# Rotary embedding on one core: loads and stores change queues, and the late loads wait between ScalarE's copies

## Chip, cores, metric

One core of a Trainium2 chip (trn2). The metric is the device time of one execution in microseconds (us), lower is better.

## The reference

```python
# x: (16, 512, 1024) float32, cos and sin: (512, 32), num_heads = 16
x = x.reshape(batch, seq, num_heads, head_dim)          # heads of 64
x1, x2 = x[..., :32], x[..., 32:]
rotated = concatenate([x1*cos - x2*sin, x1*sin + x2*cos], axis=-1)
```

33.5 MB are read and 33.5 MB are written, with three operations per element between them.

## The kernel before, as far as the change touches it

The kernel cuts the input into 64 "rows" of 128 partitions x 1024 floats and ten transfers ("tiles"): batches 0, 1, 14 and 15 alone (4 rows each), the other twelve in pairs (8 rows each). A ring of slots in SBUF, the on-chip memory, holds 40 rows; a row is computed in place and stored from its slot. So six loads can start at once, and four (rows 40 to 47, 48 to 55, 56 to 59, 60 to 63) reuse slots and must wait for a store.

Per row, VectorE multiplies by cos into PSUM, the memory that TensorE adds into (three slots), GpSimd makes the product of the swapped halves with sin into SBUF (in the fourth row of each pair: VectorE), and the sum is made by VectorE, or, in 21 rows, by TensorE adding into PSUM and ScalarE copying the result to the slot.

```python
        def on_sync(sp):                       # SyncE: all loads
            for t, (b, n) in enumerate(tiles):
                if b * R1 % R2 == 0 and b * R1 >= RING:
                    k = (b * R1 - RING) // R2
                    sp.wait_ge(sem_out[k], 16 * stores_of(k))
                sp.dma_start(in_sbuf(t), in_dram(x1, x2, t)).then_inc(sem_in[t], 16)
                ...                            # after the first: the two tables
            sp.wait_ge(sem_rest, ...)

        def on_scalar(ae):                     # ScalarE: tables, copies, all stores
            ...
            for u in range(NU):
                t, r, k = where(u)
                if PE2[u]:
                    ae.wait_ge(sem_e, n_pe[u])
                    ae.activation(xs[:, k, :], t1_ps[:, u % NT1, :], COPY).then_inc(sem_a, 1)
                if r == tiles[t][1] - 1:
                    wait_added(ae, u)
                    k = u // R2
                    ae.dma_start(in_dram(o1, o2, t), in_sbuf(t)).then_inc(sem_out[k] if k < EARLY else sem_rest, 16)

            # VectorE's product of row u waits until PSUM slot u % 3 is free:
                    if PE2[v]:                 # v = u - 3
                        ve.wait_ge(sem_a, n_pe[v])
```

## Time and profile before

| | before |
|---|---|
| timed, median | 161.3 us |
| profiled run | 167.47 us (span 166.1) |
| bytes moved, mean rate over the profiled span | 67.26 MB, 405 GB/s |
| busy: GpSimd, VectorE, TensorE, ScalarE | 136.6, 130.5, 72.6, 24.0 us |

The profiled run was 3.8% above the timed ones. In rows of busy tenths each digit is one of 40 equal slices of the span, 9 is 90% or more. A timeline line reads: start, duration, engine, line of the program, operation, and in brackets the idle time before it and what ended it. "ACTq" and "SPq" are the queues that issue transfers. A transfer lands when the last part of its completion is in. "Room" is idle time that a delay can use up before anything after it moves.

### The profile page before, as it was taken

Reading aid. Unit: us, or ns where it says so; the run is one execution under the profiler, and the core shown is the slowest. Engines: PE = TensorE matmul, PEld = TensorE weight load, DVE = VectorE, ACT = ScalarE, POOL = GpSimd, SP = SyncE. Lnnn points to the kernel's source line nnn. Section 1 sums busy time; section 2 is a strip of 40 time slices with the busy share of each in tenths; the row PEclk is TensorE's granted clock in tenths of the full one; section 3 lists DMA queues with packets and bytes.
Section 4 is the critical chain, followed back from the end, with each engine's and each line's share of the span. In section 5 each row is a group of like instructions: output and inputs, shape, how many; then the busy total and the mean of one; then the engine's idle time right before and its main releaser. Section 6 shows DMA issues by size and latency. Waiting matters only on the chain.

```text
span 166.1 us, 568 instructions
## 1 busy us (share of the span) xinstructions
PE 72.6 (44%) x94; PEld 24.6 (15%) x94; DVE 130.5 (79%) x117; ACT 24.0 (14%) x26; POOL 136.6 (82%) x67
## 2 busy tenths in 40 slices
PE   6040006196629371924292909381193827800000
PEld 1020002041202011301130213020130212200000
DVE  0069997798999999999999899972999997069600
ACT  3020000204022201222022011302022022110000
POOL 5059999999999999999999799962999999069500
PEclk9999999957696975599659555955559555595555
DMA  5999999999999999999989999999999999999293
GB/s 158 427 425 458 450 391 426 462 391 418 446 489 387 444 434 403 482 363 412 466 387 482 395 403 466 395 442 426 403 478 426 387 422 458 442 395 434 107 383 142
DMA packets 3170, 67.26 MB, mean 405 GB/s; under 512 B 352, under 2 KB 608, under 8 KB 608
## 3 DMA queue, kind: packets, MB, share of 16 engines
q1 hardware_dynamic: 1728, 33.69, 48.3%
q10 hardware_dynamic: 1440, 33.56, 47.3%
q14 instruction: 2, 0.02, 0.0%
HBM read 33.69 MB, written 33.55 MB: 405 GB/s over the span
## 4 chain that ended last, share of the span: by engine, by line
DMA 52%; POOL 15%; issue 11%; DVE 8%; PE 6%; ACT 1%; SPq 1%; POOLq 0%; DVEq 0%; ACTq 0%
DMA x_sb<-in_x_dram 33%; DMA out_dram<-x_sb 19%; POOL t_sb L254 15%; PE t_ps L209 6%; DVE x_sb L301 4%; DVE t_ps L290 4%; ACT x_sb L175 1%; SPq L156 1%; SPq L159 1%; DVE t_sb L283 0%; DVEq L300 0%; POOLq L145 0%; POOLq L143 0%; ACTq L136 0%
## 5 line engine op out<-in xcount | busy, mean ns | idle before, releaser
L254 POOL TENSOR_TENSOR t_sb<-x_sb,s_sb 128x1024 f32<-128x1024 f32 x58 | 134.2, 2355 | 18.7 <-DMA x_sb<-in_x_dram 11.7
L209 PE MATMUL t_ps<-t_sb,ident 128*128 128x512 f32 x84 | 67.8, 966 | 65.3 <-POOL t_sb L254 45.1
L290 DVE TENSOR_TENSOR t_ps<-x_sb,pair_ps 128x1024 f32<-128x1024 f32 x48 | 57.9, 1222 | 8.1 <-DMA x_sb<-in_x_dram 4.8
L301 DVE TENSOR_TENSOR x_sb<-t_ps,t_sb 128x1024 f32<-128x1024 f32 x43 | 52.4, 1220 | 2.7 <-POOL t_sb L254 2.5
L209 PEld LDWEIGHTS t_ps<-t_sb,ident 128*128 128x128 f32 x84 | 22.7, 295 | 109.6 <-issue 62.1
L175 ACT ACTIVATE x_sb<-t_ps 128x1024 f32<-128x1024 f32 x21 | 21.5, 1024 | 112.0 <-PE t_ps L209 112.0
L290 DVE TENSOR_TENSOR t_ps<-x_sb,tab_ps 128x1024 f32<-128x1024 f32 x16 | 19.3, 1222 | 7.1 <-DMA x_sb<-in_x_dram 6.7
L283 DVE TENSOR_TENSOR t_sb<-x_sb,tab_ps 128x1024 f32<-128x1024 f32 x6 | 7.3, 1215 | 0.0
L261 DVE COPY tab_ps<-stage 128x128 f32<-128x128 f32 x1 | 0.3, 295 | 8.1 <-DMA stage<-in_cos_dram 8.1
L192 PE MATMUL pair_ps<-stage,pick 128*128 128x256 f32 x4 | 2.0, 664 | 5.6 <-DMA stage<-in_sin_dram 5.6
L185 PE MATMUL t_ps<-zero 128*128 128x512 bf16 x6 | 2.7, 630 | 1.3 <-DVE zero L259 1.3
L192 PEld LDWEIGHTS pair_ps<-stage,pick 128*128 128x128 f32 x4 | 1.2, 322 | 6.6 <-issue 6.4
L235 POOL TENSOR_SCALAR_AFFINE_SELECT pick<-pick 128x128 f32<-128x128 f32 x2 | 1.4, 706 | 0.1
L165 ACT ACT_TABLE_LOAD x1 | 1.3, 1283 | 0.8 <-PEq L334 0.8
L165 ACT ACTIVATE s_sb<-stage 128x128 f32<-128x128 f32 x1 | 0.3, 309 | 7.4 <-DMA stage<-in_sin_dram 7.4
L185 PEld LDWEIGHTS t_ps<-zero 128*128 128x128 bf16 x6 | 0.7, 137 | 2.4 <-DVE zero L259 1.2
L259 DVE MEMSET zero<- 128x256 uint32 x1 | 0.3, 272 | 0.9 <-PEq L334 0.9
L169 ACT ACTIVATE s_sb<-pair_ps 128x256 f32<-128x256 f32 x1 | 0.4, 384 | 1.7 <-PE pair_ps L192 1.7
L220 POOL MEMSET ident<- 128x128 f32 x1 | 0.2, 205 | 0.3 <-POOLq L334 0.3
L170 ACT ACTIVATE s_sb<-pair_ps 128x256 f32<-128x256 f32 x1 | 0.4, 377 | 0.0
L222 POOL TENSOR_SCALAR_AFFINE_SELECT ident<-ident 128x128 f32<-128x128 f32 x1 | 0.3, 297 | 0.1
L334 POOL MEMSET const-float32-0.0<- 128x1 f32 x1 | 0.1, 99 | 0.3 <-issue 0.3
(7 smaller groups left out, 1.3 us busy)
## 6 DMA issues: line engine op xcount, KB each, us to landing
x_sb<-in_x_dram SPq DMA_DIRECT2D x6, 4096.0 KB, 39.3
out_dram<-x_sb ACTq DMA_DIRECT2D x6, 4096.0 KB, 30.4
x_sb<-in_x_dram SPq DMA_DIRECT2D x4, 2048.0 KB, 24.3
out_dram<-x_sb ACTq DMA_DIRECT2D x4, 2048.0 KB, 17.6
stage<-in_cos_dram SPq DMA_DIRECT2D x1, 64.0 KB, 8.0
stage<-in_sin_dram SPq DMA_DIRECT2D x1, 64.0 KB, 7.7
```

What stands on the lines that cost most here:

```text
L156: sp.dma_start(in_sbuf(t), in_dram(x1, x2, t)).then_inc(sem_in[t], 16)
L159: sp.dma_start(stage[:, i, :], table.rearrange("(s r) d -> s (r d)", r=R1)).then_inc(sem, 16)
L165: ae.activation(s1_sb[:, :, 0, :], sv, COPY, scale=-1.0)
L175: ae.activation(xs[:, k, :], t1_ps[:, u % NT1, :], COPY).then_inc(sem_a, 1)
L185: pe.matmul(t1_ps[:, k, b * BANK:(b + 1) * BANK], zero[:, 0:P], zero[:], start=True, stop=True).then_inc(sem_w, 1)
L192: pe.matmul(pair_ps[:, k].rearrange("p c r d -> p (c r d)"), pick[:, k].rearrange("q s b -> q (s b)"), stage[:].rearrange("q c f -> q (c f)"),
L209: ins = pe.matmul(t1_ps[:, u % NT1, b * BANK:(b + 1) * BANK], ident[:], t2[:, b * BANK:(b + 1) * BANK], start=False, stop=True, skip_group ...
L235: pl.affine_select(out=pick[:, k], in_=pick[:, k], compare_op=mybir.AluOpType.is_equal, fill=0.0, base=-k, pattern=[[-2, P // 2], [0, 2]], ...
L254: pl.tensor_tensor(t2_sb[:, u % NT2, :, :, :], swapped(k), over_heads(s_of(t, r)), mult).then_inc(sem_p, 1)
L283: ve.tensor_tensor(t2_sb[:, u % NT2, :, :, :], swapped(k), over_heads(v_ps), mult)
L290: ve.tensor_tensor(t1_ps[:, u % NT1, :].rearrange("p (h d) -> p h d", d=HALF), x_sb[:, k, :, :, :].rearrange("p h t d -> p (h t) d"), c_of ...
L301: ve.tensor_tensor(xs[:, k, :], t1_ps[:, u % NT1, :], t2_sb[:, u % NT2, :, :, :].rearrange("p h t d -> p (h t d)"), add,).then_inc(sem_v, 1)
```

## The change

Intent: swap the two queues, so that the engine with no arithmetic (SyncE) issues each store the moment its rows are ready, and ScalarE, which only has copies, issues the loads. The late loads and their waits come into ScalarE's program after the copy of the row that lies LAG = 10 rows behind the last row of the store that frees the slots. That is after rows 17, 25 and 33 (two loads).

```diff
+    LAG = 10
         def on_sync(sp):
+            for u in range(NU):
+                t, r, k = where(u)
+                if r == tiles[t][1] - 1:
+                    wait_added(sp, u)
+                    ...
+                    sp.dma_start(in_dram(o1, o2, t), in_sbuf(t)).then_inc(...)
         def on_scalar(ae):
+            later = {}
             for t, (b, n) in enumerate(tiles):
-                    sp.wait_ge(sem_out[k], 16 * stores_of(k))
+                if b * R1 + n <= RING:
+                    load(ae, t)
+                else:
+                    later.setdefault((b * R1 - RING) // R2 * R2 + R2 - 1 + LAG, []).append(t)
             ...
             for u in range(NU):
                 if PE2[u]:
                     ...                              # the copy, as before
-                if r == tiles[t][1] - 1:             # the store, now on SyncE
+                for t in later.get(u, ()):
+                    k = (tiles[t][0] * R1 - RING) // R2
+                    ae.wait_ge(sem_out[k], 16 * stores_of(k))
+                    load(ae, t)
```

No instruction of the other three engines changes.

More of the change, by code (lines that the diff above doesn't have):

```diff
@@ L149, in stores_of, with load, on_scalar @@
             return sum(b * R1 // R2 == k for b, _ in tiles)
+        def load(eng, t):
+            eng.dma_start(in_sbuf(t), in_dram(x1, x2, t)).then_inc(sem_in[t], 16)
         def on_sync(sp):
+            for u in range(NU):
+                t, r, k = where(u)
+                if r == tiles[t][1] - 1:
+                    wait_added(sp, u)
+                    k = u // R2
+                    sp.dma_start(in_dram(o1, o2, t), in_sbuf(t)).then_inc(sem_out[k] if k < EARLY else sem_rest, 16)
+            sp.wait_ge(sem_rest, 16 * sum(stores_of(k) for k in range(EARLY, NU // R2)))
+        def on_scalar(ae):
+            later = {}
             for t, (b, n) in enumerate(tiles):
-                if b * R1 % R2 == 0 and b * R1 >= RING:
-                    k = (b * R1 - RING) // R2
-                    sp.wait_ge(sem_out[k], 16 * stores_of(k))
-                sp.dma_start(in_sbuf(t), in_dram(x1, x2, t)).then_inc(sem_in[t], 16)
+                if b * R1 + n <= RING:
+                    load(ae, t)
+                else:
+                    later.setdefault((b * R1 - RING) // R2 * R2 + R2 - 1 + LAG, []).append(t)
                 if t == 0:
                     for i, (table, sem) in enumerate(((cos, sem_cos), (sin, sem_sin))):
-                        sp.dma_start(stage[:, i, :], table.rearrange("(s r) d -> s (r d)", r=R1)).then_inc(sem, 16)
-            sp.wait_ge(sem_rest, 16 * sum(stores_of(k) for k in range(EARLY, NU // R2)))
-        def on_scalar(ae):
+                        ae.dma_start(stage[:, i, :], table.rearrange("(s r) d -> s (r d)", r=R1)).then_inc(sem, 16)
             ae.wait_ge(sem_sin, 16)
@@ L171, in on_scalar @@
             for u in range(NU):
-                t, r, k = where(u)
                 if PE2[u]:
                     ae.wait_ge(sem_e, n_pe[u])
-                    ae.activation(xs[:, k, :], t1_ps[:, u % NT1, :], COPY).then_inc(sem_a, 1)
-                if r == tiles[t][1] - 1:
-                    wait_added(ae, u)
-                    k = u // R2
-                    ae.dma_start(in_dram(o1, o2, t), in_sbuf(t)).then_inc(sem_out[k] if k < EARLY else sem_rest, 16)
+                    ae.activation(xs[:, u % RING, :], t1_ps[:, u % NT1, :], COPY).then_inc(sem_a, 1)
+                for t in later.get(u, ()):
+                    k = (tiles[t][0] * R1 - RING) // R2
+                    ae.wait_ge(sem_out[k], 16 * stores_of(k))
+                    load(ae, t)
         def on_tensor(pe):
```

## The prediction

> **What bounds the kernel now.** I read the page's share of busy time by slice first, then the chain of waits, then the timelines of the issuing queues, of ScalarE and of VectorE around the four late loads.
>
> The page, busy tenths by slice (40 slices of 4.15 us):
>
> ```profile
> DVE  0069997798999999999999899972999997069600
> POOL 5059999999999999999999799962999999069500
> DMA  5999999999999999999989999999999999999293
> GB/s 158 427 425 458 450 391 426 462 391 418 446 489 387 444 434 403 482 363 412 466 387 482 395 403 466 395 442 426 403 478 426 387 422 458 442 395 434 107 383 142
> ```
>
> The DMA row is full from slice 2 to slice 37, about 2 to 153 us. DVE and POOL are nearly full too, but show holes at slices 28 and 35. So the transfers lead, and the arithmetic follows with a little room. Only the last three slices are something else: a tail of arithmetic and one store.
>
> The end of that tail, from the timelines of VectorE, of GpSimd and of ScalarE's queue:
>
> ```profile
> 130.36 1.22 DVE L290 TENSOR_TENSOR t_ps<-x_sb,pair_ps 128x1024 f32<-128x1024 f32 x1
> 131.51 1.23 DVE L290 TENSOR_TENSOR t_ps<-x_sb,tab_ps 128x1024 f32<-128x1024 f32 x1
> ...
> 146.65 2.36 DVE L290 TENSOR_TENSOR t_ps<-x_sb,tab_ps 128x1024 f32<-128x1024 f32 x2 [6.66 <-DMA x_sb<-in_x_dram]
> ```
> ```profile
> 146.70 9.27 POOL L254 TENSOR_TENSOR t_sb<-x_sb,s_sb 128x1024 f32<-128x1024 f32 x4 [5.85 <-DMA x_sb<-in_x_dram]
> ```
>
> The last load (batch 15, rows 60 to 63) is complete at 146.65. VectorE had stood idle 6.66 us for it and GpSimd 5.85. After it come four GpSimd products (9.27 us), one addition (1.22) and the last store, issued at 157.38 and complete at 166.02. So the span is the landing of the last load plus 19.4 us, and the room in front of it is 5.85 us on GpSimd.
>
> **What the change touches.** The kernel holds 40 of 64 rows. Four loads reuse slots: batches 10 and 11 (rows 40 to 47), 12 and 13 (48 to 55), 14 (56 to 59) and 15 (60 to 63). They wait for the stores of rows 0 to 7, 8 to 15 and, the last two, 16 to 23. The queue's own waits on SyncE and its timeline give the moments:
>
> ```profile
> SPq L156 <- DMA out_dram<-x_sb: 88.3, 3, 49.6
> ```
> ```profile
> 55.21 0.54 SPq L156 DMA_DIRECT2D x_sb<-in_x_dram  x1
> ```
> ```profile
> 75.55 0.53 SPq L156 DMA_DIRECT2D x_sb<-in_x_dram  x1
> ```
> ```profile
> 94.96 1.48 SPq L156 DMA_DIRECT2D x_sb<-in_x_dram  x2
> ```
>
> SyncE waits 88 us in all, which is free, as it has nothing else to do; every late load starts as soon as its store has landed. In the new kernel ScalarE does these waits, between copies that other engines need. Its timeline now (copies are of rows 6, 9, 11, 14, 17, 19, 22, 25, 27, 30, 33, 35 and so on, counted off in order):
>
> ```profile
> 53.05 1.02 ACT L175 ACTIVATE x_sb<-t_ps 128x1024 f32<-128x1024 f32 x1 [5.50 <-PE t_ps L209]
> 55.41 1.02 ACT L175 ACTIVATE x_sb<-t_ps 128x1024 f32<-128x1024 f32 x1 [1.34 <-PE t_ps L209]
> ...
> 69.45 1.02 ACT L175 ACTIVATE x_sb<-t_ps 128x1024 f32<-128x1024 f32 x1 [6.38 <-PE t_ps L209]
> 71.69 1.02 ACT L175 ACTIVATE x_sb<-t_ps 128x1024 f32<-128x1024 f32 x1 [1.22 <-PE t_ps L209]
> ...
> 85.63 1.02 ACT L175 ACTIVATE x_sb<-t_ps 128x1024 f32<-128x1024 f32 x1 [7.40 <-PE t_ps L209]
> 88.29 1.02 ACT L175 ACTIVATE x_sb<-t_ps 128x1024 f32<-128x1024 f32 x1 [1.64 <-PE t_ps L209]
> ```
>
> These are rows 17 and 19, 25 and 27, 33 and 35. The new waits stand after rows 17, 25 and 33, that is, in the three short gaps.
>
> **What the Trainium skill says.** "DMA: Bandwidth & Descriptors", section Issuing engines are not separate DMA queues: transfers from either engine end on the same 16 DMA engines and interleave, and a second issuer saves issue time only. The trace agrees that issue is small: 0.34 to 0.61 us on ScalarE's queue, 0.34 to 1.10 on SyncE's, for transfers that take 8 to 69 us to land. So swapping the two queues should not change the rate. The same page, section Anatomy of one DMA: a semaphore wait happens on the issuing sequencer before dispatch. "Perfetto Trace Analysis", section Tensor Engine Instruction, says that ScalarE is strictly first in, first out. Together: a ScalarE that waits for a store cannot start the next copy. The trace of before can't show that for loads, as ScalarE waits for no transfer after the tables. "ScalarE: Activation LUTs", section What ACT_TABLE_LOAD costs, gives about 1283 ns for a table load; the trace has 1.28 us.
>
> **The change part by part.**
>
> Removed: ten store issues from ScalarE, about 0.5 us each (5 us). None delayed a copy: every idle stretch of a copy is put down to TensorE (112.0 us, 21 times). Worth 0.
>
> Start: ScalarE issues eight transfers where SyncE did, from about 0.8 us to 5.6 us. Its table load, now at 0.80, moves behind them to about 5.6 to 6.9 us; its first real work starts at 9.43, when the sine table lands. Worth 0, give or take 0.2 us.
>
> Late loads, in the profiled timing. The first: row 17 is copied at 54.07, the store lands at 55.2, so ScalarE waits 1.1 us; with 0.54 of issue, row 19 is copied at 55.8 instead of 55.41: 0.4 late, at most. The second: row 25 is copied at 70.47, landing 75.5, a wait of 5.0; row 27 at 76.1 instead of 71.69: 4.4 late. VectorE's product for row 30 reuses the PSUM slot of row 27 (three slots), and in the trace it follows that copy directly, so VectorE stops for these 4.4 us. The third: row 33, now copied at 91.1, landing 94.9, a wait of 3.8 and two issues of 1.5; row 35 at 96.4 instead of 88.29: 8.1 late in all. So the arithmetic reaches row 40 about 8 us later than before.
>
> That is then paid out of the room that it has. Before, VectorE waits 0.80 us for the load of row 40, 4.04 for row 48, none for row 56 and 6.66 for row 60. Of 8.1 us, 0.8 is absorbed at row 40, 4.0 at row 48, and 3.3 is left at row 56; it meets 6.66 us of room (5.85 on GpSimd) at row 60. Nothing reaches the end.
>
> The loads themselves (landings here are issue plus time to landing, from the list of DMA issues taken by stretches): each is issued when its store lands, or, if that has landed before the copy is done, a moment after. Reads stay queued: when the load of row 40 is issued at 55.2, the load of rows 32 to 39 is still under way until 73.8, so some 18 us of delay are free. Stores: those of rows 24 to 31 are issued at 79.7, 4.4 later now, while the one before is under way until 94.9; those of rows 32 to 39 at 96.8, 8 later, against 115.1; rows 40 to 47 at 117.4, 3.5 later, against 131.7. Neither queue runs dry. Sum: 0.
>
> **Timed against profiled.** The profiled run took 167.47 us, the timed ones 161.3. With a fixed tail, I take the last load to land some 5 us earlier when timed (about 141), with landings a proportional 3.5% earlier; the arithmetic is not faster. That is an assumption. Then stores land at 53.3, 72.9 and 91.6: no first wait, 1.9 us late after the second, about 4.8 after the third (row 35 at 93.1 instead of 88.3). Loads land near 91, 111, 127 and 141.5. Before, the arithmetic reaches row 40 at 93.5, row 48 at 110.1 (waits to 111), row 56 at 127.5 and row 60 at about 136: 5 us of room. Now row 40 at 98.3, row 48 at 115, row 56 at 131.5, row 60 at 140 to 141. The delay just fits in. From 0 to 1.5 us may come through: I take 0.3, which gives 161.6.
>
> **Rivals.** (a) ScalarE's waits come through to the end. For it: my timed estimate leaves hardly a microsecond, and the holes at rows 48 and 60 are all the room there is. If stores land as late as in the profile while the loads come as early as I assume, 3 us come through: 164 to 165. Against it: the same transfers feed both, so late stores go with late loads. (b) The new order helps: delayed arithmetic delays stores, reads get a larger share, the last load lands earlier. It would give 159 to 160. Against it: store queues are backed up by 10 to 18 us throughout. (c) The swap of queues changes how reads and writes share, for instance at the start, where ScalarE must issue before anything moves. Either way, perhaps 1 us.
>
> **Range and chances.** Repeats of before lie within 0.13 us. The mechanism says 0 with more room upward than down: 160.4 to 163.8. Faster by over 2% (under 158.1) needs a shorter transfer stream, and nothing removes bytes: 0.02. Slower by over 2% (over 164.5) needs nearly all of the ScalarE delay to arrive at the end: 0.08. The rest, 0.90.
>
> **What would show it.** In the new profile, ScalarE should show waits for stores of about 1, 5 and 4 us after rows 17, 25 and 33; VectorE should idle for ScalarE by about 8 us where it has 3.6 now; its waits at rows 40 and 48 should vanish and that at row 60 shrink to about 3 us; the last load should land within 1 us of 146.65, and the tail remain 19.4. I'm wrong if VectorE or GpSimd no longer wait at row 60, if the last load lands over 2 us earlier or later, or if slices of the DMA row before the 37th fall below 9.

## The result and the profile after

Timed 161.19 us (161.09 to 161.42, 6 runs) against 161.34 for before (6 runs): ratio 0.9991, 95% interval 0.9979 to 1.0004. The time is the same. Ratios here are the mean of one kernel's fast runs over the mean of the other's of the same rounds, so not quite the ratio of the medians. Executions over 1.5% slower than the fastest of the same kernel are left out of the means.

The profile after: span 159.8 us. Busy rows of its page:

```profile
DVE  0069998799999999987989729899989998989500
POOL 5069999999999999999999999994999999289400
DMA  5999999999999999999999999999999999999997
GB/s 144 395 458 480 394 394 431 422 509 410 394 427 427 494 418 402 451 459 404 402 468 443 394 459 451 402 435 418 418 439 472 435 402 418 492 402 435 390 447 304
```

Against the page of before, the holes of the DMA row near the end (a 2 at slice 38, a 3 at the last) are gone: the transfers are at 9 from the second slice to the one before the last. For a fair comparison I ran the unchanged kernel again (e1, span 160.0). Its page:

```profile
DMA  5999999999999999999999999999999999999996
GB/s 135 415 454 471 393 442 422 430 451 418 401 463 438 461 393 418 475 418 404 467 434 410 434 442 426 418 451 406 414 459 467 414 410 414 475 418 442 410 410 295
```

The DMA row of before is as full. What differed in the slow profile can be read from the records of completions, which come in sixteen parts for each transfer. The profile counts sixteen DMA engines; I read one part as one engine, which the records do not name. In the slow one the store of rows 40 to 47 has fifteen parts in by 142.6 us and the sixteenth at 146.8; in e1 all sixteen lie between 139.5 and 140.6. The last load shows the same: fifteen parts by 141.4 and the sixteenth at 146.6 in the slow profile, all sixteen between 138.3 and 140.3 in e1. Read so, one engine lagged, and what waits for the last part waited for it.

Where ScalarE waits now, from its timeline after:

```profile
68.96 1.02 ACT L186 ACTIVATE x_sb<-t_ps 128x1024 f32<-128x1024 f32 x1 [7.08 <-PE t_ps L220]
72.81 0.54 ACTq L153 DMA_DIRECT2D x_sb<-in_x_dram  x1
73.40 1.02 ACT L186 ACTIVATE x_sb<-t_ps 128x1024 f32<-128x1024 f32 x1 [3.42 <-DMA out_dram<-x_sb]
...
83.92 1.02 ACT L186 ACTIVATE x_sb<-t_ps 128x1024 f32<-128x1024 f32 x1 [3.34 <-PE t_ps L220]
92.18 1.45 ACTq L153 DMA_DIRECT2D x_sb<-in_x_dram  x2
93.67 1.02 ACT L186 ACTIVATE x_sb<-t_ps 128x1024 f32<-128x1024 f32 x1 [8.73 <-issue]
```

The copy of row 25 ends at 69.98 and the store of rows 8 to 15 lands at 72.8: ScalarE stands for 2.8 us, then issues the load and copies row 27 at 73.40 (71.31 in e1). After row 33 it stands from 84.94 to 92.18, 7.2 us, and row 35 is copied at 93.67 (87.94 in e1), 5.7 us late. (The profile writes the 8.73 us before that copy, which are this wait and the issue of two loads, to "issue".) After row 17 there is no wait: the load is issued at 52.93, while that copy runs.

What VectorE made of it, first in e1, then after, in their timelines (the first two lines of each); the line below them is from GpSimd's timeline:

```profile
111.25 1.23 DVE L290 TENSOR_TENSOR t_ps<-x_sb,pair_ps 128x1024 f32<-128x1024 f32 x1 [1.62 <-DMA x_sb<-in_x_dram]
...
140.32 2.36 DVE L290 TENSOR_TENSOR t_ps<-x_sb,tab_ps 128x1024 f32<-128x1024 f32 x2 [4.08 <-DMA x_sb<-in_x_dram]
```
```profile
140.37 9.27 POOL L254 TENSOR_TENSOR t_sb<-x_sb,s_sb 128x1024 f32<-128x1024 f32 x4 [3.62 <-DMA x_sb<-in_x_dram]
```
```profile
94.72 1.23 DVE L301 TENSOR_TENSOR t_ps<-x_sb,pair_ps 128x1024 f32<-128x1024 f32 x1 [3.84 <-ACT x_sb L186]
...
140.42 2.36 DVE L301 TENSOR_TENSOR t_ps<-x_sb,tab_ps 128x1024 f32<-128x1024 f32 x2 [0.61 <-DMA x_sb<-in_x_dram]
```
```profile
140.47 9.27 POOL L265 TENSOR_TENSOR t_sb<-x_sb,s_sb 128x1024 f32<-128x1024 f32 x4 [3.64 <-DMA x_sb<-in_x_dram]
```

Before, VectorE has 1.62 us of room at row 48 and 4.08 at row 60, where it waits for loads. After, it stands 3.84 us for ScalarE at row 38, has no wait at row 48 and 0.61 us left at row 60. The delay of about 5 us is paid out of the waits for loads, and the last load lands at the same time (140.3 and 140.4). GpSimd's wait for it is 3.62 and 3.64 us: it was not delayed at all.

### The profile page after: what moved, and what is told of

It reads as the page before. It is cut to its first block, busy times and chain, and to the rows that moved or that the text cites. A ratio compares the mean times of both kernels' runs of the same rounds, so it can differ in the third digit from the quotient of the medians.

```text
span 159.8 us, 568 instructions
## 1 busy us (share of the span) xinstructions
PE 70.9 (44%) x94; PEld 23.3 (15%) x94; DVE 130.6 (82%) x117; ACT 23.9 (15%) x26; POOL 136.4 (85%) x67
## 4 chain that ended last, share of the span: by engine, by line
DMA 30%; POOL 18%; issue 17%; DVE 17%; PE 8%; ACT 3%; ACTq 2%; POOLq 0%; DVEq 0%; SPq 0%
DMA out_dram<-x_sb 18%; POOL t_sb L265 18%; DMA x_sb<-in_x_dram 11%; DVE x_sb L312 8%; PE t_ps L220 8%; DVE t_ps L301 7%; ACT x_sb L186 3%; ACTq L153 1%; DVE t_sb L294 1%; ACTq L174 1%; POOLq L144 0%; POOLq L146 0%; DVEq L311 0%; DVEq L146 0%; SPq L137 0%
## 5 line engine op out<-in xcount | busy, mean ns | idle before, releaser
L220 PE MATMUL t_ps<-t_sb,ident 128*128 128x512 f32 x84 | 66.1, 940 | 64.8 <-DVE t_ps L301 34.7
L220 PEld LDWEIGHTS t_ps<-t_sb,ident 128*128 128x128 f32 x84 | 21.4, 279 | 109.2 <-DVE t_ps L301 60.2
```

Source lines behind the costliest of these rows:

```text
L220: ins = pe.matmul(t1_ps[:, u % NT1, b * BANK:(b + 1) * BANK], ident[:], t2[:, b * BANK:(b + 1) * BANK], start=False, stop=True, skip_group ...
```

## Experiments

Theories. **A**: the sixteen DMA engines are the floor. They are busy from the first load to the last byte of the last store, so what the other engines lose costs nothing until a queue of transfers runs dry. **B**, as the prediction had it: the end is the landing of the last load plus 19.4 us of arithmetic and one store, and the room is the idle time before that arithmetic. **C**: the change of queues gains something that ScalarE's waits cost. All runs are timed against before on the same chip.

**e1, before again.** No edit.

> The kernel before, unchanged, for a profile in the fast state and for the noise of a comparison with itself. Ratio 1.000 within 0.002. Theory A (the 16 DMA engines are the floor, busy to the last byte): the profile shows a full DMA row to the last slice, as in the profile after, the last load landing near 140.4 and stores landing one right after another up to the end. Theory B (the end is the last load's landing plus a tail of arithmetic and one store, 19.4 us): holes in the DMA row between the arithmetic and the last store, as in the slow profile of before. Both: VectorE waits 4 to 6 us for the last load at row 60, against 0.61 in the profile after.

161.40 us, ratio 1.0004 (0.9991 to 1.0017). The profile is above: the full DMA row is theory A's; the room of 4.08 us at row 60 both theories expected. One of its five runs was slow (163.98).

**e2, the waits without the change of queues.** Before, and:

```diff
+                if u in (17, 25, 33):
+                    j = (u - 17) // R2
+                    ae.wait_ge(sem_out[j], 16 * stores_of(j))
                 if r == tiles[t][1] - 1:
                     wait_added(ae, u)
```

> The kernel before, whose ScalarE also waits for the stores of rows 0 to 7, 8 to 15 and 16 to 23 after its copies of rows 17, 25 and 33, while SyncE still issues all loads and ScalarE all stores. Theories A and B (the waits are absorbed): 161.2 to 161.5, with ScalarE waits of about 3.5 and 8 us and a VectorE wait at row 60 that falls to about 1 us. Theory C (the change of queues gains what the waits cost): slower than before, 161.8 or more, as the waits are there without the gain.

161.36 us, ratio 1.0000 (0.9988 to 1.0012). ScalarE waits 11.1 us for stores in two waits, and VectorE's room at row 60 falls from 4.08 to:

```profile
140.44 2.36 DVE L293 TENSOR_TENSOR t_ps<-x_sb,tab_ps 128x1024 f32<-128x1024 f32 x2 [1.58 <-DMA x_sb<-in_x_dram]
```

The waits alone cost nothing. C falls.

**e3, the change of queues without the waits.** After, with `LAG = 14`.

> The kernel after with a distance of 14 rows instead of 10: the late loads stand after rows 19, 27 and 35 are copied and before rows 22, 30 and 38, so that ScalarE should wait less than 2 us in all. Theories A and B: 161.1 to 161.4, no gain, although VectorE no longer waits for ScalarE by 3.84 us and has several us of room at row 60 again. Theory C: faster, 160.6 or less, as the gain of the queues is left without the waits.

161.20 us, ratio 0.9997 (0.9985 to 1.0009). No wait of a copy is put down to a store any more; VectorE has its room again and nothing comes of it:

```profile
140.42 2.36 DVE L301 TENSOR_TENSOR t_ps<-x_sb,tab_ps 128x1024 f32<-128x1024 f32 x2 [4.57 <-DMA x_sb<-in_x_dram]
```

**e5, no arithmetic at all.** After, without the programs of GpSimd, TensorE and VectorE and without ScalarE's copies; a store waits for its load. Its output is wrong, which doesn't matter for the time.

```diff
-                    wait_added(sp, u)
+                    sp.wait_ge(sem_in[t], 16)
```

> All arithmetic taken out of the kernel after: the same loads and stores of the same sizes on the same queues with the same ring of 40 rows, each store waiting for its load alone. The result is wrong on purpose (an unrotated copy). Theory A (the 16 DMA engines are the floor): 160.5 to 161.5, as both kernels. Theory B (the last load's landing plus 19.4 us of tail): the 10.6 us of arithmetic after the last load are gone, so 151 to 156.

161.25 us, ratio 0.9991 (0.9978 to 1.0003), and the same full row:

```profile
DMA  5999999999999999999999999999999999999997
```

A bare copy with these transfers and this ring takes as long as the whole kernel. That is the floor, measured. The order of the traffic is another one: stores are issued earlier, the last load lands only at 151.5 instead of 140.4, and the end stays at 160.0, 8.5 us after that landing and not 19.4. It also rules out that anything on the compute engines makes this kernel faster, unless the transfers change.

**e6, less arithmetic after the last load.** After, with rows 61 to 63 left out of the arithmetic (`SKIP = [u >= NU - 3 ...]` in the three engines' loops and counts). Its output is wrong, which doesn't matter for the time.

> The kernel after without the arithmetic of rows 61 to 63 (stored as loaded; the result is wrong on purpose), so that some 7 us of the arithmetic after the last load are gone and the last store can be issued near 144 instead of 151.14. Theory A: 161.0 to 161.4, as the store ahead of it lands only near 154.9 in any case. Theory B: 154 to 156.

161.26 us, ratio 0.9990 (0.9977 to 1.0002). The last store is issued near 144 instead of 151.14 and lands at 159.9 all the same. B falls: the 10.6 us of arithmetic in the "tail" are not on the path.

**e7 and e11, more arithmetic after the last load.** After, with GpSimd's product of the last row made once, or three times, more (each waits for the one before it):

```diff
+                if u == NU - 1:
+                    for again in range(1):          # e11: range(3)
+                        pl.tensor_tensor(t2_sb[...], swapped(k), ..., mult).then_inc(sem_x, 1)
+                        pl.wait_ge(sem_x, again + 1)
```

> The kernel after with GpSimd's product of the last row made twice, 2.4 us more of arithmetic after the last load; the last store is issued near 153.5. Theory A: the store ahead lands between 154.1 and 154.9, so the new one comes just in time or a little late: 161.2 to 162.2. Theory B: 163.4 to 163.8.

> GpSimd's product of the last row made four times, 7.1 us more of arithmetic after the last load: the last store is issued near 158.2, when all stores ahead have landed (154.9). Its own time alone is then what is left, 5 us of data and about 2 us more: a span of 165 to 166, so 166.3 to 167.4 timed. Theory A: the room after the last load is about 3 us, between one repeat (nothing, 161.35) and this. If the end were free of the last store's issue, it would stay at 161.3; theory B: 168.2.

e7: 161.35 us, ratio 1.0001 (0.9988 to 1.0015). e11: 166.12 us, ratio 1.0292 (1.0277 to 1.0307), with a span of 164.6, a little under what I expected. The last store's issue and its time to landing, in the timeline of SyncE's queue and in the list of DMA issues, for after, e7 and e11:

```profile
151.14 0.34 SPq L161 DMA_DIRECT2D out_dram<-x_sb  x1
...
out_dram<-x_sb SPq DMA_DIRECT2D x1, 2048.0 KB, 8.6
```
```profile
153.51 0.34 SPq L162 DMA_DIRECT2D out_dram<-x_sb  x1
...
out_dram<-x_sb SPq DMA_DIRECT2D x1, 2048.0 KB, 6.3
```
```profile
158.26 0.34 SPq L162 DMA_DIRECT2D out_dram<-x_sb  x1
...
out_dram<-x_sb SPq DMA_DIRECT2D x1, 2048.0 KB, 6.3
```

Alone, the last store takes 6.3 us (e11). In after it takes 8.6, as it stands behind the store of rows 56 to 59. So it may be issued at 159.74 - 6.3 = 153.4 without cost, 2.3 us later than it is. e7 issues it at 153.51, right at that edge, and costs nothing; e11 issues it 4.9 us past the edge, and its span is 4.8 us longer. So the room at the end, for a delay of GpSimd, is its wait of 3.64 us plus 2.3 (a sum; no run tests both parts at once).

**e4 and e8, longer waits.** After, with `LAG = 8` and `LAG = 6`.

> The kernel after with a distance of 8 rows: now row 17, not row 19, is copied only after the first store has landed (52.9), row 25 not before 72.8, row 33 not before 92.2; row 33 was copied at 83.92 with distance 10. So row 33 stands where row 35 stood, and the arithmetic is 3 to 4.5 us later from row 36 on. Theory B: room at row 60 is 0.6 us on VectorE and 3.64 on GpSimd, so 1 to 3.5 us come through: 162 to 164.7. Theory A: the last store was issued 3.8 us before the store ahead of it had landed (151.14 against 154.9), which is room too: 161.1 to 162.2.

> Distance 6: row 14 is copied only after the first store has landed (53), 8 us later than now, and row 15 is in the next store, which is then issued only after the first has landed. From here on a wait feeds the next one: row 22 waits for that store (landing near 76), row 30 for the one after (near 98), where row 30 is now copied near 79. Arithmetic about 20 us late at row 30 leaves no room: theories A and B both 172 to 180, with holes in the store queue around 54 and 77. Were the waits not what costs, it would stay near 162.

e4: 161.84 us, ratio 1.0026 (1.0006 to 1.0046). The fast runs scatter, from 161.28 to 162.41. VectorE stands 3.0 and 4.8 us for ScalarE and never waits for a load again; its room is used up, GpSimd has 1.08 us of 3.64 left, and yet only 0.5 us come through (median). In its profile the last store is issued at 152.67, before the edge, so it isn't the end of the arithmetic that costs. The stores of rows 40 to 47 and 48 to 55 are issued at 121.77 and 137.96, only 2.8 and 1.3 us before the first engine starts the completion of the store ahead (124.6 and 139.3); in after they are issued at 117.21 and 134.05. e9 shows what so short a lead does. The first of the two agrees in its packets: they start at 125.8 to about 128 us, at 125.3 to 126.0 in after, and it lands 0.7 us later (141.3 against 140.6); the last store lands 1.0 later. The second shows no such gap. That this is the cause here is argued, not shown by a run.

e8: 178.47 us, ratio 1.1039 (1.0991 to 1.1088). ScalarE's waits for stores in e8:

```profile
ACT x_sb L186 <- DMA out_dram<-x_sb: 45.3, 3, 16.6
```

Here the wait closes a circle. The copy that waits for a store belongs to the very next store, so that one is issued only after the first has landed (55.30 after 53.6, 81.78 after 80.1, 105.80 after 103.9), and store time and arithmetic add up instead of overlapping. Between distances 8 and 6 lies the edge.

**e9, e10 and e12, later loads.** After, with `LAG = 18`, `26` and `16`.

> Distance 18: late loads are issued after the copies of rows 25, 33 and 41, near 70, 86 and 102, always after the store that they wait for has landed, so ScalarE waits for no store at all. The load ahead of each is still under way until 72.6, 92 and 111.3, so the reads don't run dry. Theory A: 161.1 to 161.5. If a late load had to start as soon as its slot is free, its 17, 12 and 9 us of delay would show: 165 or more.

> Distance 26: the late loads are issued after the copies of rows 33, 41 and 49, the first near 86, while the load ahead of it has landed at 72.6. Reads stand still for some 14 us, the load of row 40 lands between 101 and 106 instead of 92, and the chain behind it moves by about as much. Theory A, whose condition (no queue runs dry) is broken here: 163 to 170, about 165. If the transfers only had to add up, whatever their order, it would stay below 162.

> Distance 16: the late loads are issued after the copies of rows 22, 30 and 38, the first near 62.5, some 9 us before the load ahead of it has been read (its completions were started from 71.3 on), where distance 18 issued it at 68.9, 2.4 us before, and its first packets started at 73.3 to 75.7. If what cost time at distance 18 is a lead shorter than the 4.4 us and more from issue to first packet, this one costs nothing: 161.1 to 161.5, and the load of row 40 lands at 92 as before. If any delay of the late loads costs, 9 us of it should show as a part of the 1.4 us of distance 18: 161.8 or more.

e9: 162.82 us, ratio 1.0095 (1.0061 to 1.0129), its runs from 161.98 to 163.95, all above the highest fast run of before (161.74). I had expected nothing. The first late load is issued at 68.91, and GpSimd waits for it until 96.05, though the load lands at 92.0 in after, where it was issued at 52.93:

```profile
96.05 16.22 POOL L265 TENSOR_TENSOR t_sb<-x_sb,s_sb 128x1024 f32<-128x1024 f32 x7 [3.35 <-DMA x_sb<-in_x_dram]
...
144.56 9.27 POOL L265 TENSOR_TENSOR t_sb<-x_sb,s_sb 128x1024 f32<-128x1024 f32 x4 [3.68 <-DMA x_sb<-in_x_dram]
```

The issue of the first late load in ScalarE's timeline, in e9 and, for comparison, in e12:

```profile
68.91 0.54 ACTq L153 DMA_DIRECT2D x_sb<-in_x_dram  x1
```
```profile
60.92 0.54 ACTq L153 DMA_DIRECT2D x_sb<-in_x_dram  x1
```

In the packets of the load queue of e9, the load ahead starts its completions at 71.3 to 72.1, and the first fourteen data packets of the late load start at 73.3 to 75.7: 4.4 to 6.8 us after issue, and the load queue moves no data in between. In after such packets follow at once (71.4 on). Meanwhile the store queue moves its own packets. Other transfers issued onto an empty queue beside a busy one show the same: 3.9 us to the first packet for the first store of after (20.18 to 24.08), 5.1 to 5.3 us for the late loads of e10. With nothing else under way it is 0.8 us (last store of e11, 158.26 to 159.10). The loads stay 4 us behind: the last one lands at 144.5 instead of 140.4. Of these 4.1 us, 2.3 are the room of the last store, and 1.8 come through, in a span of 161.6 against 159.8. The second and third late loads, issued 12 us after their slots are free but still about 7 us before the load ahead is through, lose nothing more.

e12: 161.25 us, ratio 0.9994 (0.9980 to 1.0008). The first late load is issued at 60.92, 7 us after its slot is free and 9 us before the first engine is through with the load ahead, and costs nothing. So delay as such is free; a lead of 2.4 us is too short.

e10: 174.96 us, ratio 1.0832 (1.0816 to 1.0849), worse than my 163 to 170. I had counted one standstill of reads; each late load waits for rows that need the late load before it, so there are three, and GpSimd waits 22.1 us for loads in all.

## Why the prediction was right

The time (161.6 predicted, 161.19 measured) and the class were right. Step by step:

- **Removed issues worth 0, start worth 0.** Right. ScalarE issues its first load at 0.81 us, SyncE did at 0.80; the table load moves to 5.44 to 6.72 us, and ScalarE's first real work still waits 2.25 us for the sine table.
- **Swap of the queues worth 0.** Right, shown by e3: the rate over the span is 421 GB/s against 420 in e1.
- **ScalarE's waits and the delay.** The timed version of the sum held: no first wait; row 27 expected 1.9 us late, measured 2.1; row 35 expected 4.8 late, measured 5.7. The waits named as signs for a profile (1, 5 and 4 us) were those of the slow profile's timing; measured were 0, 2.8 and 7.2. That ScalarE starts no copy while it waits for a store, which the prediction took from the skill (from a section headed as the GpSimd path) and the trace of before could not show, the last two waits show. VectorE's idle time for ScalarE came out as named: 8.3 us (e1: 3.5). One sign of being wrong came true to the letter, as the last load landed at 140.4 and not near 146.65; e1 shows that this is the state of the profile and not the change (140.3). The third wait was mis-sized because row 33 was not late: its copy starts at 83.92, in e1 at 85.34. TensorE's four matmuls for it took 1.99 us where e1 has them in a run of eight of 6.35 us, and they waited for VectorE and not for GpSimd; why they were quicker is not shown. So ScalarE was early at the wait and stood there longer; the copy after it is bound to the store's landing in any case.
- **The delay is absorbed.** Right, and shown by e2. VectorE's room at row 60 was predicted to be used up nearly entirely; it went from 4.08 to 0.61 us. But the prediction's chief rival, that a little more would come through to the end, rested on the next step, which was wrong.
- **"So the span is the landing of the last load plus 19.4 us."** The sum fits after (140.40 + 19.34 = 159.74), but as a cause it failed: take 7 us out of it (e6), and the end does not move; take all arithmetic out (e5), likewise. In the fast state the stores are backed up to the end, so the tail is store traffic. I took the holes in the slow profile's last slices for the kernel's structure; as read above, they came from one late DMA engine. (In the slow run itself the last store was issued with little ahead of it, and the sum may hold there; no run tests that.) The room at the end is larger than the prediction's, by the 2.3 us of e7 and e11. The number held although this step was wrong because the delay was used up before it came to the step; that much was luck.
- **"Some 18 us of delay are free" for the loads.** Wrong in size: 16 us (slot free at 52.9, issue at 68.91, e9) cost 1%, 7 us (e12) nothing. The transfer must be issued several us before the queue is through, not just before it.
- **Neither queue runs dry.** Right for this change. But the store queue is not "backed up by 10 to 18 us throughout": in the slow profile a store is issued 3.8 (the last) to 18.3 us before the one ahead of it lands. Its DMA row, too, called full to slice 37, has an 8 at slice 21.

Open: why a transfer issued with little lead takes 4.4 us and more to its first packet beside a busy store queue, what sets the rate of the DMA engines, and which engine lags.

## What to carry to other kernels

When the DMA row is full from end to end, test the floor first by running the transfers without the arithmetic; if that takes as long, rearranging which engine waits gains nothing and can lose. A wait put between an engine's other work was free here as long as its delay stayed under the downstream idle time, but count whether the waited-for event lies in the same loop: at distance 10 the wait was absorbed, at 6 it closed a circle and cost 10%. And issue a transfer well before its queue runs empty while the other queue is busy: here 9 us of lead cost nothing and 2.4 us cost 1%.

## What the Trainium skill lacked or had wrong

- "DMA: Bandwidth & Descriptors", section Latency and other measured facts, gives a first byte about 600 ns after issue for these queues. Beside a busy store queue e9 shows 4.4 to 6.8 us from issue to a load's first data packet in its first fourteen packets, and 4 us lost on the load; with nothing else under way e11 shows 0.8 us. The page gives no figure for the lead that a queue needs beside a busy one.
- The same page says that engines 7 and 15 are usually slower and, as a best guess, ties it to the other way of issuing (from GpSimd). Both kernels issue from SyncE and ScalarE alone, and in the slow profile the sixteenth part of the store of rows 40 to 47 came 4.2 us after the fifteenth (146.8 against 142.6), with 1.1 us between first and last in the fast one (e1). The records do not name the engine, so whether it is 7 or 15 stays open.
- No page has that a profile can fall in such a state and then show holes at the end that a profile of the fast state does not have: 166.1 against 160.0 us of span for the same kernel.
